# A two-layer hybrid decoder trunk: rotary halves on VectorE, reloads issued by ScalarE, staged compressed probabilities, an early split of w_out's operands

## The chip, the core and the metric

The kernel runs on one core of one Trainium2 chip. What is measured is the device time of one execution in microseconds (us). The core has TensorE (PE, the matmuls; PEld is its weight load), VectorE (DVE), ScalarE (ACT), GpSimd (POOL) and SyncE (SP, which here only issues DMAs). Every engine works through its own queue in order and waits on semaphores for the others.

## What is computed

A trunk of two layers over 512 tokens of width 1024, all in float32. Each layer is a feed-forward half step, a mixing step of three attentions, and another feed-forward half step. Cut to what matters here:

```
h = x + 0.5 * swiglu(rms_norm(x, g1), w1, w3, w2)
u = rms_norm(h, g_mix);  proj = u @ w_in      # columns for A, B and C
A: dilated windows, 3 groups (window, dilation) = (128,1), (512,4), (2048,16); q and k rotated by rope
   o = sum over groups of softmax(lse)[g] * out[g]
B: p_cmp = masked_softmax(q @ kc^T); compressed, selected and window branches;
   q and k rotated by rope; sigmoid gates per branch
C: stick-breaking attention, strictly causal
y = gate0 * (o_a @ w_up_a) + gate1 * (o_b @ w_up_b) + gate2 * (o_c @ w_up_c)
h = h + y @ w_out
h = h + 0.5 * swiglu(rms_norm(h, g2), v1, v3, v2)
```

`apply_rope` turns the first 16 of 64 columns of each head: two products with cos and sin, one difference, one sum.

## The kernel before

All large products run on TensorE in fp32r with split operands: an operand is taken apart into a rounded part (hi) and the rest (lo), and one product is three matmuls, as `acc<-gh,whi`, `acc<-gl,whi`, `acc<-gh,wlo`. Weights are streamed: SP issues the load of a tile `raw` (L352), ScalarE copies it to `whi` (L358), VectorE subtracts to `wlo` (L359), and some tiles later TensorE uses both. A matmul with 512 columns is the usual one; the projection `w_in` runs some with 384.

In mixing, TensorE has two kinds of work. One is that weight stream: `w_in`, the sigmoid gates `w_gate`, then `w_up` and `w_out` (`acc` is their PSUM bank). The other are the small matmuls and transposes of the attentions (`sps` scores, `tps` transposes, `ops` outputs), cut into *units*: generators that `yield` a number of nanoseconds where their next step depends on other engines. `weave` (L426) writes TensorE's order out when the program is built: it keeps a clock of its own estimates, resumes a unit when its due time has come, and otherwise puts the next step of the weight stream (`self.step()`) there as fill. So a `yield` of 3200 means "put about 3200 ns of the weight stream here". TensorE's order is fixed that way; a scheduler then orders VectorE, ScalarE, GpSimd and SP's instructions around it. A unit that is not yet ready (`need`) holds all units behind it in the pending list.

Names that the following needs:

- `rope` (L667 to L681): `ra`, `rb` products with cos and sin, then difference and sum into the first 16 columns. Called on `nata` (A's q and k, 128 partitions), `natk` and `natq` (B's).
- `c_unit` (L843): stick breaking; GpSimd masks `e` and `f` (L851), VectorE scans `f` (L853), GpSimd multiplies `e<-e,f` (L854), TensorE transposes `e`.
- `b_cmp_probs` (L1186 to L1203): the compressed probabilities `ec` of head group g (0 or 1): add the mask, max, subtract, exp, mask again on GpSimd (L1191), sum (L1192), reciprocal, scale on GpSimd (L1196), then transposes.
- The scores of B's other branches are evacuated by VectorE at L1219 (`e,sm<-sps`), normalised by GpSimd at L1223 and transposed.
- `a_unit`: A's attention of one group; softmax sums are put through the small matmuls `tps<-asm,selT` and `tps<-ay,sel`, the group weights `ad`, `ay` (L1438) and `aw` (L1459) come from VectorE, `ea` is scaled (L1443) and transposed, `pa` is its evacuated transpose (L1492).
- The dilated groups store `nata` and `va` to HBM (`ag`) and load them in another layout: `nata<-ag` (L1335) and `va<-ag` (L1336), three reloads in each layer; tile `nat` has two buffers.
- `merge` (L953): `gt` is the stored gate, loaded back by SP (L964), then `gt<-gt,acc` (L969) and `y<-y,gt` (L970). `project_out` splits `y` into `yh` (ScalarE, L988) and `yl` (VectorE, L989) as the operands of `w_out`.

Of the kernel before, what the change touches and what calls it, by code (L numbers as in the profile page):

```python
# [8 lines left out]
F32 = mybir.dt.float32  # L9
F32R = mybir.dt.float32r  # L10
I32 = mybir.dt.int32
AF = mybir.ActivationFunctionType
ALU = mybir.AluOpType
# [42 lines left out]
class Trunk:  # L56
# [610 lines left out]
    def rope(self, x, dil, H):  # L667

        nc = self.nc
        c0 = 4 if dil else 0  # L670
        shp = [128, 4, H, 16]
        cos = self.cos[:, c0:c0 + 4, None, :].to_broadcast(shp)
        sin = self.sin[:, c0:c0 + 4, None, :].to_broadcast(shp)
        ta, tb = self.et("ra"), self.et("rb")
        a = ta[:, :64 * H].rearrange("p (t h d) -> p t h d", t=4, h=H)
        b = tb[:, :64 * H].rearrange("p (t h d) -> p t h d", t=4, h=H)
        xr = x[:, :, :, 0:16]
        nc.gpsimd.tensor_tensor(a, xr, cos, op=ALU.mult)
        nc.gpsimd.tensor_tensor(b, xr, sin, op=ALU.mult)  # L679
        nc.gpsimd.tensor_tensor(x[:, :, :, 0:8], a[:, :, :, 0:8], b[:, :, :, 8:16], op=ALU.subtract)  # L680
        nc.gpsimd.tensor_tensor(x[:, :, :, 8:16], a[:, :, :, 8:16], b[:, :, :, 0:8], op=ALU.add)  # L681

    def st(self, dt, name):
        return self.mp.tile([128, 512], dt, tag="st", name=name, bufs=12)
# [268 lines left out]
    def merge(self, l, mx, r0, o, ready):  # L953
        nc = self.nc
        for mq in range(4):
            ts = []

            def out(j, ts=ts):
                ts.append(self.gt())
                return ts[-1]  # L960

            def load(mq=mq, ts=ts):
                for j in range(2):
                    nc.sync.dma_start(out(j, ts), self.gates[mx, mq][:, j, :])  # L964

            def post(ps, mq=mq, ts=ts):
                for j in range(2):
                    y = self.y[2 * mq + j]
                    nc.vector.scalar_tensor_tensor(ts[j], ts[j], 1.0, ps[j], op0=ALU.add, op1=ALU.mult)  # L969
                    (nc.gpsimd if mx else nc.vector).tensor_tensor(y, y, ts[j], op=ALU.add)  # L970
                if mq == 3:
                    self.done.add(("merge", l, mx))

            if (mx, mq) in self.gates:
                yield self.up(l, r0, mq, o, post, lambda mq=mq: ready(mq), load)
            else:
                yield self.gate(l, mx, mq, out, lambda mq=mq: ready(mq))
                yield self.up(l, r0, mq, o, post)

    def project_out(self, l):  # L980
        nc = self.nc
        yh, yl, h = [], [], []

        def pre():
            for k in range(KD):
                hi = self.gp.tile([128, 512], F32R, tag="gh", name="yh")
                lo = self.gp.tile([128, 512], F32R, tag="gl", name="yl")
                nc.scalar.activation(hi, self.y[k], AF.Copy)  # L988
                nc.vector.tensor_tensor(lo, self.y[k], hi.bitcast(F32), op=ALU.subtract)  # L989
                yh.append(hi)  # L990
                yl.append(lo)

        for mq in range(4):
            def post(ps, mq=mq):
                for j in range(2):
                    m = 2 * mq + j
                    t = self.rp.tile([128, 512], F32, tag="hr", name="hr", bufs=2)
                    nc.sync.dma_start(t, self.spill[:, m, :])
                    hn = self.hp.tile([128, 512], F32, tag="h", name="h")
                    nc.vector.scalar_tensor_tensor(hn, ps[j], 0.5, t, op0=ALU.mult, op1=ALU.add)  # L1000
                    h.append(hn)
                    self.stat_add(m, hn)
                if mq == 3:
                    self.h = h
                    self.done.add(("out", l))

            yield self.proj(self.ins["w_out"][l], 0, (4, 4), mq * 256, lambda: (yh, yl), post,
                            pre=pre if mq == 0 else None,
                            ready=lambda: ("merge", l, 0) in self.done and ("merge", l, 1) in self.done)


# [150 lines left out]
    def b_cmp_probs(self, l, g):  # L1162
        nc = self.nc

        def make(U):
            b, mp = self.b, self.mp
            qt = []
            for p in (2 * g, 2 * g + 1):
                ps = self.trans4(lambda j: b["q"][p][:, j, :])
                t = self.st(F32, "qt")  # L1170
                nc.scalar.activation(t, ps, AF.Copy)
                qt.append(t)
                yield "", 2000 * 0.5
                self.rope(b["q"][p].rearrange("p t (h d) -> p t h d", d=64), False, 2)
            yield "", 2000
            ps = self.sps()
            for i in range(4):
                for p in range(2):
                    self.mm(ps[:, i * 128 + p * 64:i * 128 + (p + 1) * 64], qt[p][:, i * 128:(i + 1) * 128],
                            b["kc"][:, g].rearrange("p a c -> p (a c)"), start=True, stop=True)  # L1180
            e = self.et("ec")
            ev = e.rearrange("p (i r c) -> p i r c", i=4, r=4)
            shp = [128, 4, 4, 32]
            small = lambda n: mp.tile([128, 4, 4], F32, tag=n, name=n, bufs=1)
            mx, ls = small("cmx"), small("cls")
            nc.vector.tensor_tensor(ev, ps.rearrange("p (i r c) -> p i r c", i=4, r=4),  # L1186
                                    self.MC[:, :, None, :].to_broadcast(shp), op=ALU.add)
            nc.vector.tensor_reduce(mx, ev, axis=AX.X, op=ALU.max)
            nc.vector.tensor_tensor(ev, ev, mx[:, :, :, None].to_broadcast(shp), op=ALU.subtract)
            nc.scalar.activation(e, e, AF.Exp)  # L1190
            nc.gpsimd.tensor_tensor(ev, ev, self.MC1[:, :, None, :].to_broadcast(shp), op=ALU.mult)  # L1191
            nc.vector.tensor_reduce(ls, ev, axis=AX.X, op=ALU.add)  # L1192
            nc.vector.tensor_scalar(ls, ls, 1e-30, None, op0=ALU.max)
            nc.vector.reciprocal(ls, ls)
            nc.vector.tensor_tensor(ls, ls, b["g"][:, :, 4 * g:4 * g + 4, 0], op=ALU.mult)
            nc.gpsimd.tensor_tensor(ev, ev, ls[:, :, :, None].to_broadcast(shp), op=ALU.mult)  # L1196
            self.done.add(("cq", l, g))
            yield "", 9200
            ps = self.trans4(lambda i: e[:, i * 128:(i + 1) * 128])
            ph = mp.tile([128, 512], F32R, tag="pch", name="pch", bufs=1)  # L1200
            pl = mp.tile([128, 512], F32R, tag="pcl", name="pcl", bufs=1)
            nc.scalar.activation(ph, ps, AF.Copy)
            nc.vector.tensor_tensor(pl, ps, ph.bitcast(F32), op=ALU.subtract)  # L1203
            b["pc"][g] = ph, pl

        def need():
            d = self.done
            return ("cmp", l) in d and ("bk", l, 1) in d and (g == 0 or ("cqfree", l) in d)

        return Unit(make, need=need, tiles=3)  # L1210
# [119 lines left out]
    def a_reload(self, l, p):  # L1330
        nc = self.nc
        a = self.ain[p]
        a["nat"][0] = self.mp.tile([128, 4, 256], F32, tag="nat", name="nata", bufs=2)
        a["v"][0] = self.mp.tile([128, 2, 4, 128], F32, tag="v2", name="va", bufs=3)[:, 0]
        nc.sync.dma_start(a["nat"][0], self.ag0[p][0])  # L1335
        nc.sync.dma_start(a["v"][0], self.ag0[p][1])  # L1336
        self.done.add(("ag0", l, p))

# [33 lines left out]
    def a_unit(self, l, p):  # L1372
        nc = self.nc

        def make(U):
# [75 lines left out]
            for ip in range(2):  # L1451
                for h in range(2):
                    weigh(0, h, ip)
            yield "", 3200
            ps = self.tps()
            for i in range(4):
                self.mm(ps[:, 0:8], self.sel[:, i, :], y[:, i].rearrange("p c h -> p (c h)"), start=(i == 0),
# [96 lines left out]
    def mix_jobs(self, l):  # L1554
        self.y, self.oc, self.ob, self.oa = [], self.obs.setdefault((l, "c"), []), self.obs.setdefault(l, []), []
        self.gates = {}
        self.gd, self.gld = [], []
        self.cin, self.ain, self.O, self.b, self.ag0 = {}, {}, {}, {"qs": {}, "pc": {}}, {}
        has = lambda *f: (lambda: f in self.done)
        for p in range(3):  # L1560
            yield self.c_inputs(l, p)
        yield from self.b_inputs(l)
        yield from self.a_natural(l)
        for p in range(3):
            yield from self.a_inputs(l, p)
        yield from self.merge(l, 0, 0, {"n": 3, "t": self.oa}, lambda mq: ("adone", l) in self.done)
        yield from self.project_out(l)
# [149 lines left out]
```

## Time and profile before

| | us |
|---|---|
| median of 3 runs | 2831.61 (2830.56 to 2831.69) |
| the profiled execution, its own time | 2828.33 |
| its span in the trace | 2826.6 |
| PE busy | 2777.8 (98%) |
| DVE busy | 1485.0 (53%) |
| ACT busy | 1174.5 (42%) |
| POOL busy | 514.8 (18%) |
| mean granted TensorE clock | 0.996 |

The profiled execution has 1.7 us outside its span, and is 3.3 us below the median. Layer 0's mixing lies between about 450 and 1030 us, layer 1's between 1850 and 2426 us; the rest is feed-forward.

### The profile page before, as it was taken

How to read it: one execution, taken by the hardware profiler on the slowest of the kernel's cores; microseconds unless marked ns; L12 is line 12 of the kernel's file. 1: busy time of each engine (PE TensorE's matmuls, PEld its weight loads, DVE VectorE, ACT ScalarE, POOL GpSimd, SP SyncE). 2: the span in 40 equal slices, each digit the busy share in tenths (PEclk: the TensorE clock that was granted, in tenths of full speed). 3: DMA queues.
4: the chain of work that ended last, by engine and by line, in shares of the span. 5: the costliest groups of instructions: out<-in, count | busy, mean ns of one | idle time of the engine just before them, and what ended most of it. 6: DMA issues, size and time to landing. Idle time of an engine off the chain costs nothing.

```text
span 2826.6 us, 39056 instructions
## 1 busy us (share of the span) xinstructions
PE 2777.8 (98%) x14281; PEld 2387.1 (84%) x14281; DVE 1485.0 (53%) x2923; ACT 1174.5 (42%) x2427; POOL 514.8 (18%) x637
## 2 busy tenths in 40 slices
PE   8999999999999999999999999999999999999998
PEld 7888898888988888888888888988889887888886
DVE  5464346566754565443354543565666446654433
ACT  4333345455644333333233332554556444433332
POOL 2120022133311231110011100231333112311100
PEclk9999999999999999999999999999999999999999
DMA  4333332322233243332333333323222333433332
GB/s 128 97 98 99 117 88 86 95 88 77 69 108 101 86 149 97 97 97 90 104 90 97 97 104 109 88 90 106 77 72 81 97 108 105 128 97 97 97 96 76
DMA packets 298576, 274.58 MB, mean 97 GB/s; under 512 B 14616, under 2 KB 278928, under 8 KB 298384
## 3 DMA queue, kind: packets, MB, share of 16 engines
q1 hardware_dynamic: 292608, 264.49, 31.7%
q10 hardware_dynamic: 5776, 7.60, 0.8%
q8 instruction: 112, 1.84, 0.3%
q14 instruction: 80, 0.66, 0.1%
HBM read 253.69 MB, written 18.35 MB: 96 GB/s over the span
## 4 chain that ended last, share of the span: by engine, by line
PE 92%; DVE 2%; ACT 1%; POOL 1%; issue 1%; DMA 1%; SPq 0%; DVEq 0%; ACTq 0%; POOLq 0%
PE acc L82 64%; PE tps L82 9%; PE sps L82 8%; PE ops L82 8%; PE tps L102 4%; DVE wlo L359 1%; ACT whi L358 0%; DMA gt<-gate 0%; DMA nata<-ag 0%; DMA raw<-in_w_in_dram 0%; POOL ec L1191 0%; POOL e L854 0%; POOL ss L292 0%; DVE ea L1443 0%; POOL rb L679 0%
## 5 line engine op out<-in xcount | busy, mean ns | idle before, releaser
L359 DVE TENSOR_TENSOR wlo<-raw,whi 128x512 fp32r<-128x512 f32 (+3 forms) x944 | 654.1, 700 | 885.2 <-ACT whi L358 835.7
L358 ACT ACTIVATE whi<-raw 128x512 fp32r<-128x512 f32 (+3 forms) x944 | 560.8, 601 | 1031.4 <-PE acc L82 768.8
L82 PE MATMUL acc<-gh,whi 128*128 128x512 f32 x928 | 364.4, 393 | 0.0
L82 PE MATMUL acc<-gh,wlo 128*128 128x512 f32 x928 | 361.6, 390 | 0.0
L82 PE MATMUL acc<-gl,whi 128*128 128x512 f32 x928 | 361.4, 389 | 0.0
L530 POOL TENSOR_TENSOR a<-a,Rb 128x512 f32<-128x512 f32 x88 | 129.6, 1498 | 906.4 <-DVE a L529 877.0
L82 PE MATMUL acc<-hh,whi 128*128 128x512 f32 x704 | 274.2, 390 | 0.0
L82 PE MATMUL acc<-hh,wlo 128*128 128x512 f32 x704 | 273.9, 389 | 0.0
L82 PE MATMUL acc<-hl,whi 128*128 128x512 f32 x704 | 273.9, 389 | 0.0
L82 PEld LDWEIGHTS acc<-gh,wlo 128*128 128x128 f32 x928 | 174.2, 188 | 36.7
L82 PE MATMUL acc<-whi,gh 128*128 128x384 f32 (+2 forms) x576 | 204.4, 355 | 0.0
L82 PEld LDWEIGHTS acc<-gh,whi 128*128 128x128 f32 x928 | 174.4, 188 | 34.9
L82 PEld LDWEIGHTS acc<-gl,whi 128*128 128x128 f32 x928 | 174.4, 188 | 34.7
L82 PE MATMUL acc<-wlo,gh 128*128 128x384 f32 (+2 forms) x576 | 198.3, 344 | 0.5 <-DVE wlo L359 0.5
L82 PE MATMUL acc<-whi,gl 128*128 128x384 f32 (+2 forms) x576 | 197.9, 344 | 0.0
L82 PEld LDWEIGHTS acc<-hh,wlo 128*128 128x128 f32 x704 | 132.1, 188 | 27.5
L82 PEld LDWEIGHTS acc<-hl,whi 128*128 128x128 f32 x704 | 132.2, 188 | 27.3
L82 PEld LDWEIGHTS acc<-hh,whi 128*128 128x128 f32 x704 | 132.1, 188 | 27.3
L82 PE MATMUL acc<-whi,gd 128*128 128x384 f32 x384 | 135.1, 352 | 0.0
L82 PE MATMUL acc<-wlo,gd 128*128 128x384 f32 x384 | 129.5, 337 | 0.0
L82 PE MATMUL acc<-whi,gld 128*128 128x384 f32 x384 | 129.2, 337 | 0.0
L82 PE MATMUL tps<-gh,whi 128*128 128x512 f32 x320 | 124.5, 389 | 0.0
(377 smaller groups left out, 5427.7 us busy)
## 6 DMA issues: line engine op xcount, KB each, us to landing
raw<-in_ffn_w_dram SPq DMA_DIRECT2D x256, 512.0 KB, 3.7
raw<-in_w_in_dram SPq DMA_DIRECT2D x288, 128.0 KB, 2.4
raw<-in_w_gate_dram SPq DMA_DIRECT2D x48, 512.0 KB, 3.5
raw<-in_w_in_dram SPq DMA_DIRECT2D x16, 512.0 KB, 3.6
raw<-in_w_out_dram SPq DMA_DIRECT2D x16, 512.0 KB, 3.6
gate<-gt ACTq DMA_DIRECT2D x28, 256.0 KB, 2.0
gt<-gate SPq DMA_DIRECT2D x28, 256.0 KB, 3.1
raw<-in_w_up_dram SPq DMA_DIRECT2D x16, 384.0 KB, 3.2
```

The costliest lines, as they stand in the source:

```text
L82: self.nc.tensor.matmul(out, lhsT, rhs, start=start, stop=stop, **kw)
L102: self.nc.tensor.transpose(out, in_, self.ident[:n, :n])
L358: nc.scalar.activation(hi, x, AF.Copy)
L359: nc.vector.tensor_tensor(lo, x, hi.bitcast(F32), op=ALU.subtract)
L530: nc.gpsimd.tensor_tensor(v[j], v[j], self.Rb, op=ALU.mult)
```

## The change

Five edits, all in mixing:

1. `rope`: of four GpSimd instructions, the product with sin (L679) and the sum (L681) go to VectorE.
2. `merge` counts its merges per pair of y tiles; after the second one it calls the new `y_split` for that pair. Before, `project_out` made all eight splits as it began.
3. `b_cmp_probs`, for head group 1 only: three new yields (2000, 2500, 2500) between its steps, and the last becomes 4000; group 0 keeps 9200.
4. the reload of `nata` is issued by ScalarE's queue rather than SP's.
5. `a_unit`: a yield of 4200 where 3200 stood, before `tps<-ay,sel`.

```
-        nc.gpsimd.tensor_tensor(b, xr, sin, op=ALU.mult)
+        nc.vector.tensor_tensor(b, xr, sin, op=ALU.mult)
         nc.gpsimd.tensor_tensor(x[:, :, :, 0:8], a[:, :, :, 0:8], b[:, :, :, 8:16], op=ALU.subtract)
-        nc.gpsimd.tensor_tensor(x[:, :, :, 8:16], a[:, :, :, 8:16], b[:, :, :, 0:8], op=ALU.add)
+        nc.vector.tensor_tensor(x[:, :, :, 8:16], a[:, :, :, 8:16], b[:, :, :, 0:8], op=ALU.add)
...
+                self.merged[mq] += 1
+                if self.merged[mq] == 2:
+                    for j in range(2):
+                        self.y_split(2 * mq + j)
...
+    def y_split(self, k):
+        nc = self.nc
+        hi = self.gp.tile([128, 512], F32R, tag="gh", name="yh")
+        lo = self.gp.tile([128, 512], F32R, tag="gl", name="yl")
+        nc.scalar.activation(hi, self.y[k], AF.Copy)
+        nc.vector.tensor_tensor(lo, self.y[k], hi.bitcast(F32), op=ALU.subtract)
+        self.yh[k], self.yl[k] = hi, lo
...
             nc.vector.tensor_reduce(mx, ev, axis=AX.X, op=ALU.max)
+            if g:
+                yield "", 2000
             nc.vector.tensor_tensor(ev, ev, mx[:, :, :, None].to_broadcast(shp), op=ALU.subtract)
             nc.scalar.activation(e, e, AF.Exp)
+            if g:
+                yield "", 2500
             nc.gpsimd.tensor_tensor(ev, ev, self.MC1[:, :, None, :].to_broadcast(shp), op=ALU.mult)
+            if g:
+                yield "", 2500
             nc.vector.tensor_reduce(ls, ev, axis=AX.X, op=ALU.add)
...
-            yield "", 9200
+            yield "", 4000 if g else 9200
...
-        nc.sync.dma_start(a["nat"][0], self.ag0[p][0])
+        nc.scalar.dma_start(a["nat"][0], self.ag0[p][0])
...
-            yield "", 3200
+            yield "", 4200
```

What the order of the instructions becomes is shown at three places.

GpSimd's queue, layer 0, the last unit of stick breaking (`e`, `f`) beside the second rotation of `natk`; before:

```order
L854 TENSOR_TENSOR e<-e,f 128x383
L678 TENSOR_TENSOR ra<-natk,cos 128x256
L851 AFFINE_SELECT f<-f 128x128
L679 TENSOR_TENSOR rb<-natk,sin 128x256
L851 AFFINE_SELECT e<-e 128x128
L680 TENSOR_TENSOR natk<-ra,rb 128x16x8
L681 TENSOR_TENSOR natk<-ra,rb 128x16x8
L854 TENSOR_TENSOR e<-e,f 128x511
```

The same place after:

```order
L854 TENSOR_TENSOR e<-e,f 128x383
L678 TENSOR_TENSOR ra<-natk,cos 128x256
L851 AFFINE_SELECT f<-f 128x128
L851 AFFINE_SELECT e<-e 128x128
L680 TENSOR_TENSOR natk<-ra,rb 128x16x8
L854 TENSOR_TENSOR e<-e,f 128x511
```

Two instructions have left GpSimd's queue ahead of the last `e<-e,f`. VectorE's queue at that place after:

```order
L359 TENSOR_TENSOR wlo<-raw,whi 128x512
L679 TENSOR_TENSOR rb<-natk,sin 128x256
L853 SCALAR_TENSOR_TENSOR f<-f 128x512
L681 TENSOR_TENSOR natk<-ra,rb 128x16x8
L359 TENSOR_TENSOR wlo<-raw,whi 128x512 x2
L766 TENSOR_TENSOR pzl<-tps,pzh 128x384
```

They stand there around the scan of `f` on which that `e<-e,f` waits.

VectorE's queue, layer 0, the compressed probabilities `ec` of head group 1; before:

```order
L1186 TENSOR_TENSOR ec<-sps,MC 128x512
L1188 TENSOR_REDUCE cmx<-ec 128x16
L703 TENSOR_TENSOR qs<-tps,qs 64x512
L1189 TENSOR_TENSOR ec<-ec,cmx 128x512
L1219 ISA e,sm<-sps,Mbig 128x128
L1219 ISA sm 128x1
L703 TENSOR_TENSOR qs<-tps,qs 64x512
L1219 ISA e,sm<-sps,Mbig 128x256
L1219 ISA sm 128x1
L359 TENSOR_TENSOR wlo<-raw,whi 128x384
L1192 TENSOR_REDUCE cls<-ec 128x16
```

After (L1186 has become L1188, L1192 L1200, L1219 L1227):

```order
L1188 TENSOR_TENSOR ec<-sps,MC 128x512
L1190 TENSOR_REDUCE cmx<-ec 128x16
L359 TENSOR_TENSOR wlo<-raw,whi 128x384 x2
L1193 TENSOR_TENSOR ec<-ec,cmx 128x512
L1274 TENSOR_SCALAR gt<-acc,r 128x128 x2
L1200 TENSOR_REDUCE cls<-ec 128x16
L1274 TENSOR_SCALAR gt<-acc,r 128x128
L359 TENSOR_TENSOR wlo<-raw,whi 128x384 x2
```

The score evacuations no longer stand between the steps of `ec`; the first one, L1227, comes ten rows behind L1200. On TensorE, 51 matmuls of 384 columns now stand between `sps<-kc,qt` (which makes `ec`) and the next attention unit, where none stood before.

TensorE's queue, layer 0, the third reload of `nata`; before (SP issues the reload behind the first row's four transposes, and its tile is read by the last eight of the sixteen):

```order
L102 MATMUL tps<-ident,nata 128x128 x4
L82 MATMUL acc<-oh,whi 128x512
L82 MATMUL acc<-ol,whi 128x512
L82 MATMUL acc<-oh,wlo 128x512
L102 MATMUL tps<-ident,nata 128x128 x16
```

After, the four transposes that free the buffer are followed by twelve matmuls `acc<-oh` and `acc<-ol`, and then by:

```order
L102 MATMUL tps<-ident,ea 128x128 x8
L82 MATMUL ops<-pa,va 64x128 x8
L102 MATMUL tps<-ident,nata 128x128 x4
L82 MATMUL ops<-pa,va 64x128 x8
L102 MATMUL tps<-ident,nata 128x128 x12
```

The last eight of the twelve read the reload. ScalarE's queue around its issue, after:

```order
L1368 ACTIVATE qa<-tps 128x512
L358 ACTIVATE whi<-raw 128x512
L1500 ACTIVATE pa<-tps 128x512
L1343 DMA nata<-ag_6374 128x1024
L358 ACTIVATE whi<-raw 128x512
L1500 ACTIVATE pa<-tps 128x512
```

The `pa` ahead of the issue comes from transposes that stand ahead of the freeing four. In a_unit, the matmuls of the weight stream between `tps<-asm,selT` and `tps<-ay,sel` become 27 where 21 stood in the first group, and 21 where 15 stood in the third. The splits `yh`, `yl` (L988, L989) keep their places between the merges on ScalarE and VectorE, but for the last pair.

## Rows read from the trace of the kernel before

**Rows 1.** The page: busy time of each engine (share of the span, instructions).

```profile
PE 2777.8 (98%) x14281; PEld 2387.1 (84%) x14281; DVE 1485.0 (53%) x2923; ACT 1174.5 (42%) x2427; POOL 514.8 (18%) x637
```

**Rows 2.** PE's waits: waiter, whom for, us in total, times, longest.

```profile
PE sps L82 <- DVE sm L1219: 5.8, 8, 1.7
PE tps L102 <- POOL e L854: 4.8, 2, 2.4
PE tps L102 <- DMA nata<-ag: 4.0, 2, 2.2
...
PE tps L102 <- POOL e L1223: 2.7, 2, 1.4
PE tps L82 <- DVE ay L1438: 1.8, 3, 0.8
PE tps L102 <- DVE aw L1459: 1.5, 3, 1.0
PE acc L82 <- DVE gt L969: 1.3, 1, 1.3
```

**Rows 3.** By stretch: length, busy PE, PEld, DVE, ACT, POOL, clock, DMA share, GB/s.

```profile
450.00:1030.00 580.00, 566.42 (x3386) 501.35 (x3385) 344.95 (x828) 287.13 (x686) 141.70 (x216) 1.00 0.32 94
1030.00:1440.00 410.00, 410.00 (x1826) 339.97 (x1825) 193.59 (x293) 141.66 (x229) 52.08 (x36) 1.00 0.33 99
```

**Rows 4.** Timeline of POOL, layer 0, last unit of stick breaking: start, duration.

```profile
584.11 1.18 POOL L679 TENSOR_TENSOR rb<-natk,sin 128x256 f32<-128x256 f32 x1
...
588.13 1.08 POOL L854 TENSOR_TENSOR e<-e,f 128x511 f32<-128x511 f32 x1
```

**Rows 5.** The same stretch, DVE.

```profile
582.00 1.27 DVE L359 TENSOR_TENSOR wlo<-raw,whi 128x512 fp32r<-128x512 f32 x1
...
584.61 1.76 DVE L853 TENSOR_TENSOR_SCAN f<-f 128x512 f32<-128x512 f32 x1
```

**Rows 6.** The same stretch, PE; brackets: idle before it and its releaser.

```profile
589.27 0.55 PE L102 MATMUL tps<-ident,e 128*128 128x128 f32 x3 [2.31 <-POOL e L854]
```

**Rows 7.** Groups by form: count, busy us, mean ns, idle before.

```profile
L679 POOL TENSOR_TENSOR rb<-nata,sin 128x256 f32<-128x256 f32 x18 | 15.8, 878 | 0.0
```

**Rows 8.** The same view, DVE's nearest form of two inputs.

```profile
L359 DVE TENSOR_TENSOR wlo<-raw,whi 128x256 fp32r<-128x256 f32 x16 | 6.7, 418 | 0.1
```

**Rows 9.** Timeline, layer 0, compressed probabilities of group 1, DVE.

```profile
695.65 0.69 DVE L1192 TENSOR_REDUCE cls<-ec 128x16 f32<-128x512 f32 x1 [1.18 <-POOL ec L1191]
```

**Rows 10.** The same stretch, PE.

```profile
697.96 0.50 PE L82 MATMUL sps<-kh,qs 128*128 128x512 f32 x1 [1.64 <-DVE sm L1219]
```

**Rows 11.** Timeline, layer 0, rotation of nata ahead of L1223, POOL.

```profile
735.02 0.77 POOL L681 TENSOR_TENSOR nata<-ra,rb 128x128 f32<-128x128 f32 x1
735.78 1.19 POOL L1223 TENSOR_SCALAR e<-e,sm,glog 128x256 f32<-128x256 f32 x2
```

**Rows 12.** Timeline, layer 1, a_unit of the first group, PE.

```profile
2240.64 0.71 PE L102 MATMUL tps<-ident,ea 128*128 128x128 f32 x3 [1.03 <-DVE aw L1459]
...
2245.73 1.04 PE L102 MATMUL tps<-ident,ea 128*128 128x128 f32 x8
2246.70 0.88 PE L82 MATMUL ops<-pa,va 128*64 128x128 f32 x12
```

**Rows 13.** By stretch, as rows 3: two stretches at half the clock.

```profile
947.20:950.70 3.50, 3.50 (x23) 2.85 (x22) 1.24 (x4) 0.68 (x2) 0.00 (x0) 0.51 0.68 220
...
2240.90:2244.30 3.40, 3.40 (x13) 3.40 (x12) 2.00 (x5) 0.00 (x0) 1.88 (x4) 0.50 0.49 154
```

**Rows 14.** Timeline, layer 0, third reload of nata, PE.

```profile
942.27 0.60 PE L102 MATMUL tps<-ident,nata 128*128 128x128 f32 x4
...
946.62 1.38 PE L102 MATMUL tps<-ident,nata 128*128 128x128 f32 x8 [2.19 <-DMA nata<-ag]
```

**Rows 15.** The same stretch, SP's queue.

```profile
942.95 0.34 SPq L1335 DMA_DIRECT2D nata<-ag  x1
```

**Rows 16.** Timeline, layer 0, the last merges, DVE.

```profile
1008.58 1.38 DVE L969 SCALAR_TENSOR_TENSOR gt<-gt,acc 128x512 f32<-128x512 f32 x2 [1.36 <-DMA gt<-gate]
```

More of the change, by code (lines that the diff above doesn't have):

```diff
@@ L978, in merge @@
                 yield self.up(l, r0, mq, o, post)
+    def y_split(self, k):
[5 more added lines that the diff above has]
+        self.yh[k], self.yl[k] = hi, lo
     def project_out(self, l):
         nc = self.nc
[L982 to L991, printed above, removed]
+        h = []
         for mq in range(4):
@@ L1005, in post @@
                     self.done.add(("out", l))
-            yield self.proj(self.ins["w_out"][l], 0, (4, 4), mq * 256, lambda: (yh, yl), post,
-                            pre=pre if mq == 0 else None,
+            yield self.proj(self.ins["w_out"][l], 0, (4, 4), mq * 256, lambda: (self.yh, self.yl), post,
                             ready=lambda: ("merge", l, 0) in self.done and ("merge", l, 1) in self.done)
@@ L1557, in mix_jobs @@
         self.gd, self.gld = [], []
+        self.merged, self.yh, self.yl = [0] * 4, {}, {}
         self.cin, self.ain, self.O, self.b, self.ag0 = {}, {}, {}, {"qs": {}, "pc": {}}, {}
```

## The prediction

> **What bounds the kernel now.** I read the page first, then PE's waits, then the stretches, then the timelines of single waits. TensorE is busy for 2777.8 of 2826.6 us [rows 1]. Both kernels give it the same matmuls, so an edit can only gain what TensorE idles, or what it runs at half its clock. The feed-forward stretch shows 410.00 busy of 410.00; a mixing stretch shows 566.42 of 580.00 with VectorE at 344.95 and GpSimd at 141.70 [rows 3]. So all that can be had is some 13.6 us in each of two mixing steps, less what no edit touches. The list of PE's waits [rows 2] says what ends it: score banks that VectorE frees late (5.8 us), `e` of stick breaking (4.8), the reload (4.0), `e` of the window branch (2.7), `ay` and `aw` of a_unit (1.8 and 1.5), a gate load (1.3). These seven rows make 21.9 us, and each edit is aimed near one of them. One matmul of 512 columns takes 410.00/1826 = 0.2245 us there [rows 3]; one of 384 columns is put at three quarters of that, 0.168.
>
> **Rotations on two engines.** There are 30 ropes (18 of `nata`, 8 of `natq`, 4 of `natk`), so 60 instructions leave GpSimd for VectorE. The widest group was 18 of 878 ns on GpSimd [rows 7]; for VectorE I take the nearest two-input row of that width, 418 ns [rows 8], and less for the narrow sum. That is some 20 us more for an engine that is 53% busy [rows 1].
>
> *Stick breaking (4.8 us).* GpSimd's multiply began at 588.13 and TensorE had its result at 589.27, 1.14 later [rows 4, 6]. The scan it also needs ended at 584.61 + 1.76 = 586.37 [rows 5]; in between GpSimd was rotating `natk`. With the queue clear the result could come at 586.37 + 1.14 = 587.51, a gain of 1.76. But the order puts `rb` in VectorE's queue ahead of that scan, for 0.42. I take 1.76 - 0.42 = 1.3 a layer, 2.6 in both; ends are 0 (the scan is held as long as GpSimd is relieved) and 3.5. What stays, some 1.0 a layer, is the scan.
>
> *Window branch (2.7 us).* The `e` that TensorE waited for began right behind a rope's sum of 0.77 [rows 11]; that and the `rb` before it, 0.88 by its mean [rows 7], are more than the 1.4 of one wait. They leave, but the units around it shift too, so another rope or cast may stand there. I take two thirds, 1.8; ends 0 and 2.7.
>
> *The price.* VectorE's two new instructions per rope can each wait for GpSimd's half, and behind them stand `wlo`, `pl`, `pzl` and the score evacuations that TensorE waits for. No row shows this wait. Below it is bounded by 0, above by one more wait of the 1.18 that a GpSimd half lasted beside VectorE's work [rows 4], were it to reach TensorE in four or five of the 30 ropes, 5 us. Matmuls have weight tiles in store and VectorE is idle for two fifths of mixing, so I take 1.0.
>
> The rows show the engines holding each other up: `rb` took 1.18 us against a mean of 0.88, while VectorE's `wlo` of 512 columns took 1.27, against 0.84 for twice the one of 256 columns [rows 4, 5, 7, 8]. By the Trainium skill, "SBUF — State Buffer", section "SBUF: two separate sides", a VectorE instruction with two SBUF inputs and a GpSimd instruction that reads SBUF take one shared port pair in turn, the later one waiting whole. That speaks against this edit, since the halves would run one after the other: these stretched rows agree, and by it the two gains above would be near their lower ends and the sum some 4 us smaller (an estimate). I keep the larger values, because even in turn VectorE's half is the shorter one.
>
> **Compressed probabilities in stages (5.8 us).** The cause is one queue. VectorE stood 1.18 us before the sum L1192, because GpSimd's second mask was not done [rows 9]; the score evacuation L1219 stood behind it, and TensorE waited 1.64 for the bank [rows 10]. The order now puts 51 matmuls, 51 x 0.168 = 8.6 us, between the matmuls that make `ec` and the next attention unit, with no evacuation among the `ec` steps. Eight waits make the row, the longest 1.7 [rows 2]; I take 5.0, ends 2.9 (a wait comes back elsewhere in each layer) and 5.8. The cost is fill used earlier: 11000 ns of yields where 9200 stood. I cost it at nothing, since weight matmuls remain behind it up to the last merge, and the later dry place is counted with the reload.
>
> **The yield of 4200 (3.3 us).** It adds 6 matmuls ahead of `tps<-ay,sel`: 6 x 0.168 = 1.0 in the first group and 6 x 0.2245 = 1.35 in the third. The longest wait for `ay` is 0.8 [rows 2], so I take 1.7 of 1.8. `aw` comes after that place; it is helped only because VectorE's scalings of `ea` are done earlier. Its longest wait is 1.03 [rows 12]; I take 1.0 of 1.5, ends 0 and 1.5. Together 2.7.
>
> **The reload (4.0 us).** In before the freeing transposes began at 942.27, SP issued at 942.95, TensorE had the tile at 946.62, having stood 2.19 [rows 14, 15]: 4.35 us from the first of the four to the use. After, the order has between the two, beside the four, 12 matmuls (2.7), 16 other transposes at 0.97/8 = 0.12 (1.9) and 16 `pa` matmuls at 0.88/12 = 0.07 (1.1) [rows 12]: 5.7 us and the four. That is over 1 us more than 4.35, so the stall of both layers goes: 4.0. This row of transposes without weight matmuls needs its banks evacuated one after the other, which I put at 0.3 a layer, ends 0 and 1.0. So 3.4. ScalarE pays for six issues; SP's took 0.34 each [rows 15], so 2.0 us on an engine with far more idle, with a few `whi` behind each, of which some are in store. Zero for TensorE.
>
> It is the position that pays, not the issuing engine: SP's queue held the reload back for TensorE's transposes, not for other issues. By the Trainium skill, "Trainium Kernel Development and Optimization", section "Key Constraints", transfers issued from SP and ScalarE share the same 16 DMA engines, and issuing from several engines saves issue time only. On that rule alone edit 4 is worth nothing and the stall would stay; it is a rival below.
>
> **Splitting y.** The scheduler had the splits between the merges already; ScalarE's and VectorE's rows barely move. Worth 0. The one wait there, 1.3 us in layer 0 alone, is VectorE's for the load of a gate [rows 2, 16]; the change moves other transfers around it, so I count it neither gone nor doubled: plus or minus 1.3.
>
> **The clock.** Two stretches of mixing ran at a granted clock of 0.50 and 0.51, that is 1.2 of 2.4 GHz [rows 13]: one began 0.6 us after the reload's wait of 2.19, the other 0.3 us after the wait for `aw` of 1.03. The second held 13 matmuls in 3.40 us, where 13 x 0.168 = 2.2, so 1.2 lost; the first held small ones, and loses at most half of 3.5; I take 0.8. Without the waits ahead I expect both gone: 2.0, ends 2.0 and -2.0 (two others appear).
>
> **Sum.** 2.6 + 1.8 + 5.0 + 2.7 + 3.4 + 2.0 - 1.0 = 16.5. The profiled execution took 2828.33 itself, so 2811.8 for one like it; the median of the runs stands 3.3 above that execution, so 2815.1, forecast 2815. Upper ends of all terms make 22 to 25 us (2807); lower ends all at once make no gain.
>
> **Rivals.** (a) *The ropes take turns.* VectorE holds its queue for GpSimd's halves; the gains in stick breaking and window branch go (4.4) and the price is 5 rather than 1. Gain 16.5 - 8.4 = 8.1, 2823.5. For it: the stretched rows. Against: GpSimd loses 15.8 us in one form and about as much again in the other forms, and is only 18% busy [rows 1, 7].
> (b) *The reload doesn't profit* (it does not do what it says): the transfer lands later behind `w_up` and gate loads now issued beside it, or ScalarE reaches its issue late. Then 3.4 and 0.8 go: 12.3, 2819.3. Against: over 1 us of spare by the order.
> (c) *Slower.* Each of the 60 moved instructions holds VectorE as the `wlo` was held, 1.27 - 0.84 = 0.43 us, and all of it reaches TensorE through late `wlo` and score banks: 60 x 0.43 = 26 in place of 1.0, so 26 - 17.5 = 8.5 lost, 2840. It decides from 17.5/60 = 0.29 us each reaching TensorE. Against: VectorE idles 235 of 580 us in mixing [rows 3].
> (d) *The waits only move*: every staged piece finds another late bank; within 0.2% of before, 2828.
>
> **How the numbers follow.** Forecast 0.67, (a) 0.14, (b) 0.10, (d) 0.05, (c) 0.04. About 0.2%, 5.7 us, is what a measurement of this kernel tells from no change: faster means below 2826. That holds for the forecast, for (b) and for most of (a), 0.86, and I take off 0.02 for what the listing of waits doesn't show: faster 0.84, same 0.11, slower 0.05. The range goes from 2804, a little below all upper ends, to 2828, which leaves out (c) and half of (d).
>
> **What would show it.** In the profile after: PE's waits for the score bank near 697 us and for `nata<-ag` are gone; `e` of stick breaking stays with about 1.0 us a layer; `ay` and `aw` under 1 us in all; no stretch at half clock near 947 or 2241; ropes' `rb` on VectorE near 0.4 us. I am wrong if VectorE's new instructions show long waits for GpSimd with `wlo` or L1227 behind them, if TensorE waits in the dry row of transposes before the third group, or if new waits stand where the 51 matmuls were taken from.

## The result: 22 us faster, with the score wait as long as before

| | before | changed |
|---|---|---|
| median, us | 2831.09 (2827.19 to 2834.06, 6 runs) | 2808.82 (2806.47 to 2809.73, 6 runs) |
| the profiled execution, its own time | 2828.33 | 2808.57 |
| span | 2826.6 | 2806.9 |

The ratio is 0.9923, with a 95% interval of 0.9912 to 0.9933: 0.8% faster, 22.3 us by the medians. Forecast were 16.5 us less than before, 2815, in a range of 2804 to 2828; the time lies in the range and the direction was right.

The page of the changed kernel answers to [rows 1]; columns are busy us, share and instructions.

```profile
PE 2772.0 (99%) x14281; PEld 2385.3 (85%) x14281; DVE 1498.6 (53%) x2983; ACT 1176.3 (42%) x2427; POOL 486.2 (17%) x577
```

TensorE has the same 14281 instructions; 60 have gone from POOL to DVE, and cost 13.6 us more there and 28.6 less on POOL (the prediction had put some 20 more on DVE). PE's waits in the changed kernel answer to [rows 2]; columns are us in total, times, longest; the first row of the list, a load at the start of the kernel (6.9), is left out:

```profile
PE sps L82 <- DVE sm L1227: 5.8, 8, 1.8
PE tps L82 <- POOL ss L292: 4.2, 1, 4.2
PE acc L82 <- DVE gt L969: 1.4, 1, 1.4
PE tps L102 <- POOL e L854: 1.3, 2, 0.7
PE ops L82 <- DVE pcl L1211: 0.9, 2, 0.4
PE tps L102 <- ACT natc L1039: 0.8, 2, 0.4
PE tps L102 <- DVE qa L1366: 0.7, 2, 0.3
```

Gone from the list are `nata<-ag` (4.0), `e` of the window branch (2.7), `ay` (1.8) and `aw` (1.5); `e` of stick breaking fell from 4.8 to 1.3. In their place stands `qa` with 0.7. (`qa` are the evacuated transposes of `nata`; `ss` are the sums of squares of a norm at the start, outside mixing, 3.6 us before; `pcl` and `pch` are the low and high part of the transposed `ec`, `pl`, `ph`, `pzl` and `pzh` those of the transposed `e`; `natc` belongs to the stick-breaking branch.) The score banks, which the largest term of the forecast meant, wait 5.8 us as before. They do it elsewhere, though. The stretches of the two mixing steps, to set beside [rows 3] (length, busy PE, PEld, DVE, ACT, POOL, clock, DMA share, GB/s), changed:

```profile
450.00:1030.00 580.00, 573.53 (x3425) 509.37 (x3424) 356.96 (x865) 290.20 (x690) 134.10 (x191) 1.00 0.32 96
...
1850.00:2426.00 576.00, 571.19 (x3415) 507.36 (x3414) 357.35 (x864) 290.72 (x687) 135.41 (x188) 1.00 0.33 97
```

Layer 1 before:

```profile
1850.00:2426.00 576.00, 563.68 (x3375) 499.90 (x3374) 344.41 (x828) 286.45 (x685) 141.27 (x215) 1.00 0.32 94
```

TensorE's idle in these stretches of time went from 13.6 to 6.5 us in layer 0 and from 12.3 to 4.8 in layer 1. Now the place of the longest score wait, layer 0, timelines of PE, DVE and POOL (start, duration, then in brackets the idle before and its releaser):

```profile
722.35 0.50 PE L82 MATMUL sps<-kh,qs 128*128 128x512 f32 x1 [1.83 <-DVE sm L1227]
...
724.85 0.67 PE L82 MATMUL acc<-whi,gd 128*128 128x384 f32 x1
725.32 0.52 PE L82 MATMUL acc<-whi,gld 128*128 128x384 f32 x1
```

```profile
719.74 0.60 DVE L359 TENSOR_TENSOR wlo<-raw,whi 128x384 fp32r<-128x384 f32 x1
720.26 0.69 DVE L798 TENSOR_TENSOR ol<-of,oh 128x512 fp32r<-128x512 f32 x1
720.87 0.35 DVE L1274 TENSOR_SCALAR gt<-acc,r 128x128 f32<-128x128 f32 x1
721.13 0.69 DVE L679 TENSOR_TENSOR rb<-nata,sin 128x256 f32<-128x256 f32 x1
721.74 0.55 DVE L1227 CUSTOM_DVE_ANT_0 e<-sps,Mbig 128x384 f32<-128x384 f32 x1
```

```profile
720.74 0.80 POOL L678 TENSOR_TENSOR ra<-nata,cos 128x256 f32<-128x256 f32 x1 [0.81 <-ACT nata L1273]
```

The evacuation L1227 that would free the bank stands in DVE's queue behind a head output's `ol`, a scaling of A's `v` (which the program names `gt` there), and `rb`, the half of the rotation that the change put on DVE. `rb` lasted 0.69 us; it began while POOL's `ra` ran (720.74 to 721.54), and the last section shows what that does. TensorE stands 1.8 us here, and up to 726.6 us its matmuls of 384 columns then begin 0.32 us apart or more, where 0.17 is usual: half the clock for a while.

The stretches of [rows 13] at half the clock are gone. The first two rows here are the start of the kernel and the piece around the end of the half clock behind that wait, the third is what now follows layer 0's last reload (columns as before):

```profile
29.00:33.80 4.80, 4.80 (x13) 3.83 (x14) 1.52 (x7) 0.21 (x1) 0.00 (x0) 0.50 0.35 109
724.80:727.20 2.40, 2.40 (x10) 2.40 (x10) 1.41 (x3) 1.54 (x4) 0.77 (x1) 0.59 0.71 186
941.60:945.10 3.50, 3.50 (x28) 2.96 (x28) 2.16 (x9) 1.90 (x8) 0.00 (x0) 1.00 0.13 45
```

### The profile page after: what moved, and what is told of

Its sections match the earlier page's. It is cut to its first block, busy times and chain, and to the rows that moved or that the text cites. A ratio compares the mean times of both kernels' runs of the same rounds, so it can differ in the third digit from the quotient of the medians.

```text
span 2806.9 us, 39062 instructions
## 1 busy us (share of the span) xinstructions
PE 2772.0 (99%) x14281; PEld 2385.3 (85%) x14281; DVE 1498.6 (53%) x2983; ACT 1176.3 (42%) x2427; POOL 486.2 (17%) x577
## 4 chain that ended last, share of the span: by engine, by line
PE 95%; DVE 2%; issue 1%; POOL 1%; ACT 1%; DMA 0%; ACTq 0%; DVEq 0%; POOLq 0%
PE acc L82 66%; PE tps L82 9%; PE sps L82 8%; PE ops L82 8%; PE tps L102 4%; DVE wlo L359 0%; DMA gt<-gate 0%; POOL e L854 0%; POOL ss L292 0%; POOL ra L678 0%; DVE e L1227 0%; DMA gr<-in_cmp_pe_v_dram 0%; ACT e L1229 0%; PE acc L102 0%; DVE rb L679 0%
```

## The experiments

Theory: TensorE's order, as the yields lay it out, decides when each wait can be covered; the engine that issues a transfer or does half a rotation matters little ("position"). Rivals: the issuing engine ends the reload's wait ("engine"); the rotation halves give with one hand and take with the other ("taking turns"). Edits 1, 3, 4 and 5 were each put alone on the kernel before; edits 1, 2, 4 and 5 were each taken alone out of the changed kernel. The changed kernel without edit 3 was not run. All ratios are to the kernel before, run on the same chip. On the chips of the three groups of runs that kernel took 2831.56, 2828.61 and 2829.56 us, so kernels of different groups are compared by their ratios, whose intervals reach 3.5 to 4 us to either side where a kernel ran four or five times. The short diffs give the whole edit.

### Edit 3 alone on the kernel before

```
+            if g:
+                yield "", 2000
...
+            if g:
+                yield "", 2500
...
+            if g:
+                yield "", 2500
...
-            yield "", 9200
+            yield "", 4000 if g else 9200
```

> The kernel before with the staged yields alone (edit 3). Theory 'position': the wait for the third reload ends because these yields move TensorE's order, whoever issues the reload. Then `nata<-ag`, 4.0 us in before, is under 0.5 here though SP still issues it, the score waits near 690 to 698 us (2.8 in each layer) are gone, `e` of the window branch (2.7) mostly too, and the kernel is 8 to 13 us faster than before, 2818 to 2823. Theory 'engine': the reload's wait ends because ScalarE issues it; then 4.0 us of it stay here and the gain is 3 to 7 us, 2824 to 2828. On the new score wait of 1.8 us near 720 us in the changed kernel: if VectorE's halves of the rotation make it, it is under 0.5 here, since all of rope is on GpSimd; if the shift of units makes it, it is 1.2 or more here too.

Measured: 2812.90 us (2809.43 to 2814.24) against 2831.56; ratio 0.9931 (0.9918 to 0.9943). PE's waits of this kernel:

```profile
PE tps L102 <- POOL e L854: 4.6, 2, 2.3
PE tps L82 <- POOL ss L292: 3.6, 1, 3.6
PE sps L82 <- DVE sm L1225: 3.5, 6, 1.0
PE tps L102 <- ACT pa L1498: 1.2, 2, 0.6
...
PE tps L102 <- DVE aw L1465: 0.4, 2, 0.2
```

No row for `nata<-ag` is left, although SP issues the reload; `ay` is gone, although the yield is 3200; `e` of the window branch is gone, although GpSimd does all rotations. The gain, 18.7 us (19.5 by the ratio), is more than either theory allowed, and the ratio's interval overlaps that of the whole change (0.9912 to 0.9933). "Position" holds and was too modest. The score waits fell from 5.8 to 3.5. The new wait near 722 us is there, with GpSimd's rotation:

```profile
723.63 0.50 PE L82 MATMUL sps<-kh,qs 128*128 128x512 f32 x1 [0.99 <-DVE sm L1225]
```

That is between the two readings of the expectation: 0.99 of the 1.83 us comes from the shift of the units, and some 0.8 from something else in the changed kernel; the run without the split rotation, below, says what.

### Edit 4 alone on the kernel before

```
-        nc.sync.dma_start(a["nat"][0], self.ag0[p][0])
+        nc.scalar.dma_start(a["nat"][0], self.ag0[p][0])
```

> The kernel before with the reload issued by ScalarE alone (edit 4); TensorE's order is that of before, word for word. Theory 'position': the wait of 4.0 us for `nata<-ag` stays between 3.5 and 5, and the time is that of before within 2 us, 2829 to 2833. Theory 'engine': it falls under 1, and the time by 4 to 6 us, 2825 to 2827.

Measured: 2833.14 us (2829.34 to 2834.80) against 2831.56; ratio 1.0004 (0.9995 to 1.0013). The waits for the reload:

```profile
PE tps L102 <- DMA nata<-ag: 4.2, 2, 2.3
```

and the view of the issuing line: the six issues, and from issue to landing.

```profile
L1335 ACTq DMA_DIRECT2D nata<-ag x6: 326/326/326, 797.9 to 2346.6; - x6
...
DMA to landing us min/median/max: 3.2/3.3/3.6
```

Nothing was gained: the transfer landed as late as by SP (3.2, 3.3 and 3.5 us in before), and TensorE waited as long. "Engine" has fallen.

### Edit 5 alone on the kernel before

```
-            yield "", 3200
+            yield "", 4200
```

> The kernel before with the yield of 4200 alone (edit 5). The waits for `ay` (1.8) go under 0.3. If the longer yield also lets VectorE reach `aw` early, the wait for `aw` (1.5) and the half clock near 2241 us go too: 4 to 5 us faster, 2826 to 2827. If `aw` was not helped by it but by the other edits, 1.5 to 2 us faster, 2829, with half a clock still granted near 2241. `nata<-ag` stays near 4.0 in both.

Measured: 2826.87 us (2823.83 to 2829.66) against 2831.56; ratio 0.9985 (0.9976 to 0.9994), 4.2 us by the ratio. `ay` is no longer in the list; `aw` stays but is spread:

```profile
PE tps L102 <- DVE aw L1459: 1.5, 4, 0.6
```

The gain is that of the first case, the mechanism is not: `aw` did not get shorter in sum, its longest wait fell from 1.0 to 0.6, and layer 1's clock from 2238 to 2245 us was granted in full (1.00). What was gained in waits are 1.8 us of `ay` and 0.6 of `pa`. Whether the stretch at half clock was gained by the edit stays open: the same trace has two that the trace before lacks, at 1982 us behind a wait of 2.29 for `e` (0.54) and at 2340 behind one of 1.76 for the reload (0.52).

### Edit 1 alone on the kernel before

```
-        nc.gpsimd.tensor_tensor(b, xr, sin, op=ALU.mult)
+        nc.vector.tensor_tensor(b, xr, sin, op=ALU.mult)
...
-        nc.gpsimd.tensor_tensor(x[:, :, :, 8:16], a[:, :, :, 8:16], b[:, :, :, 0:8], op=ALU.add)
+        nc.vector.tensor_tensor(x[:, :, :, 8:16], a[:, :, :, 8:16], b[:, :, :, 0:8], op=ALU.add)
```

> The kernel before with the rotation's halves on VectorE alone (edit 1); TensorE's order is that of before. Theory 'less queue': `e` of stick breaking falls from 4.8 to 1.3 us and `e` of the window branch from 2.7 to under 1, the score waits stay near 5.8: 4 to 6 us faster, 2825 to 2827. Theory 'taking turns eats it': the score waits grow by 3 us or more as VectorE's queue is held by the halves, and the time stays within 2 us of before, 2829 to 2833. In either, VectorE's `rb` of 128x256 begun beside GpSimd's `ra` lasts until after that `ra` ends, 0.7 to 1.0 us, against 0.4 where GpSimd is idle.

Measured: 2826.61 us (2824.93 to 2828.47) against 2831.56; ratio 0.9984 (0.9975 to 0.9992), 4.5 us by the ratio. Its waits:

```profile
PE sps L82 <- DVE sm L1219: 6.7, 10, 1.7
...
PE tps L82 <- DVE ay L1438: 2.9, 4, 1.0
PE tps L102 <- DVE pzl L766: 1.5, 2, 0.8
PE tps L102 <- POOL e L854: 1.4, 2, 0.7
```

"Less queue" gave 3.4 at stick breaking and 2.7 at the window branch, and `aw` fell by 1.1; 0.9 was taken back at the score banks, 1.1 at `ay`, 1.5 at `pzl` and 0.6 at `pa`, which fits VectorE's fuller queue. Both theories are at work and the first was the larger in this order of TensorE. VectorE's `rb` of `nata` took 0.41 to 0.91 us, 0.71 in the median; 0.7 to 1.0 had been expected beside `ra`.

### The changed kernel with the reload issued by SP

The edit is that of edit 4, reversed.

> The changed kernel with the reload issued by SP again (edit 4 undone); TensorE's order is that of the changed kernel. Theory 'position': TensorE still has no wait for `nata<-ag` and the time is that of the changed kernel within 2 us, 2807 to 2811. Theory 'engine' in a weaker form (in the new order SP's queue would hold `raw` and gate loads behind the reload): 3 to 6 us slower, 2812 to 2815, with waits for `raw`, `whi` or `gt`.

Measured: 2809.99 us (2808.19 to 2810.53), ratio 0.9927 (0.9914 to 0.9941). No wait for `nata<-ag`. The landing times, of this kernel:

```profile
DMA to landing us min/median/max: 3.3/4.3/4.4
```

and of the changed one, by ScalarE:

```profile
DMA to landing us min/median/max: 3.2/4.0/4.4
```

By the ratios edit 4 is worth about 1 us, which this measurement can't tell from nothing. The transfers land later in the new order, whoever issues them, and TensorE does not wait for them.

### The changed kernel with the yield of 3200

The edit is that of edit 5, reversed.

> The changed kernel with the yield of 3200 (edit 5 undone). The staged yields alone already ended the wait for `ay`. If the edits overlap there, this is slower than the changed kernel by 0 to 2 us, 2808 to 2811, with waits for `aw` and `pa` of under 2 us; if they add up as they do on the kernel before (4.2 us there), 2812 to 2814.

Measured: 2809.83 us (2808.41 to 2810.67), ratio 0.9929 (0.9916 to 0.9941): 1.7 us by the ratios, within their intervals. `pa` (1.2) and `aw` (0.4) wait, `ay` doesn't: what edit 5 ends, edit 3 had mostly ended.

### The changed kernel with all of rope on GpSimd

The edit is that of edit 1, reversed.

> The changed kernel with all of rope on GpSimd (edit 1 undone). `e` of stick breaking goes back from 1.3 to 4.6 us; the score wait near 720 us falls from 1.8 to about 1.0 and the one near 757 from 0.7 to about 0.5, in each layer, if VectorE's halves make up that difference. Net: the rotation on two engines is worth 0.5 to 3 us here against 4 us on the kernel before, 2809 to 2812. If the score wait does not fall, the halves are not its cause and the net is 3 to 5 us, 2812 to 2814.

Measured: 2809.33 us (2807.30 to 2809.48), ratio 0.9925 (0.9913 to 0.9938), some 0.6 us off the changed kernel by the ratios. Its waits:

```profile
PE tps L102 <- POOL e L854: 4.7, 2, 2.4
...
PE sps L82 <- DVE sm L1227: 3.5, 6, 1.0
```

The score waits fall to 3.5: VectorE's halves make 2.3 of their 5.8 us. They pay 3.4 at stick breaking, so 1.1 us of waits is left to edit 1: in the new order, it is as a whole worth nothing that could be measured. The half clock does not decide it: this trace has two such stretches, at 589 and 1975 us behind the waits for `e`, the changed kernel's has one, at 724. No row for `e` of the window branch is left here, so with edit 3 in, edit 1 is not needed for it.

### The changed kernel with all splits of y at the start of w_out

```
-                self.merged[mq] += 1
-                if self.merged[mq] == 2:
-                    for j in range(2):
-                        self.y_split(2 * mq + j)
...
+        def pre():
+            for k in range(KD):
+                self.y_split(k)
...
+                            pre=pre if mq == 0 else None,
```

> The changed kernel with all eight splits of y made as `project_out` begins (edit 2 undone). By the prediction's working it is worth nothing: 2807 to 2811, the one wait at the first matmul of w_out staying that of VectorE for a gate load, between 0 and 2.7 us in one of the layers. If the early split matters, TensorE waits for `yh` or `yl` there in both layers and the kernel is 2 to 4 us slower.

Measured: 2809.27 us (2807.18 to 2810.19), ratio 0.9926 (0.9914 to 0.9939). Edit 2 is worth nothing that could be measured, and no wait for `yh` or `yl` is in the list.

### The longer sum without the stages, on the kernel before

```
-            yield "", 9200
+            yield "", 11000 if g else 9200
```

> The kernel before with one yield of 11000 for head group 1 where 9200 stood: the same sum as edit 3, without its stages. TensorE's order at the third reload stays that of before. If the gain of the staged yields comes from the stages, which hold the next units back and so move TensorE's order, this is worth under 2 us, 2829 to 2832, with `nata<-ag` near 4.0 and the score waits near 690 to 698 us as before. If it comes from the 1800 ns more, 8 us or more faster, under 2824.

Measured: 2829.89 us (2826.65 to 2831.60) against 2829.56, ratio 0.9998 (0.9989 to 1.0007). `nata<-ag` waits 4.3 us, the score banks 8.0. So it is the stages and not the 1800 ns more: in `b_cmp_probs` the flag that lets the next unit start is set behind the new yields, so TensorE does its w_in matmuls first, and every later unit meets another piece of the weight stream. That the flag is what matters is read from the program; one long yield ahead of the flag, without stages, was not run.

### The changed kernel with the split rotation for `natk` and `natq` only

```
+    def rope(self, x, dil, H, eng=None):
...
+        eng = eng or nc.gpsimd
...
+        eng.tensor_tensor(b, xr, sin, op=ALU.mult)
...
+        eng.tensor_tensor(x[:, :, :, 8:16], a[:, :, :, 8:16], b[:, :, :, 0:8], op=ALU.add)
```

`natk` and `natq` are called with VectorE, `nata` without.

> The changed kernel with rope on two engines for `natk` and `natq` alone; all four instructions for `nata` are on GpSimd. Theory: VectorE's halves pay at stick breaking (the wait for `e` near 587 us stays at 0.7 in each layer) and cost at the score banks, by those of `nata`. Then the score waits go back to 3.5 us in all (1.0 near 720, 0.5 near 757) and the kernel is 2 to 4 us faster than the changed one, 2805 to 2807. If the score waits stay at 5.8, the halves of `nata` are not their cause and the time stays at 2808 to 2810.

Measured: 2803.86 us (2802.37 to 2807.68, 4 runs), ratio 0.9910 (0.9897 to 0.9924), against 0.9923 (0.9912 to 0.9933) of the changed kernel. By the ratios it is 3.7 us faster than the changed kernel, within the 2 to 4 that were expected, and its median is the lowest of all here; the intervals overlap, so that it beats the changed kernel is likely and not settled. The trace shows the mechanism that was foreseen:

```profile
PE sps L82 <- DVE sm L1228: 3.4, 6, 1.0
PE tps L102 <- POOL e L855: 1.3, 2, 0.7
```

### That kernel, with group 0 staged too

```
-            if g:
-                yield "", 2000
+            yield "", 2000
...
-            yield "", 4000 if g else 9200
+            yield "", 4000
```

The two yields of 2500 lose their `if g` as well.

> The kernel rope_split_for_b_only with the staged yields for head group 0 too. If staging is good in itself, the waits near 614 to 619 us (score bank 0.3, `pch` 0.2, `pcl` 0.4 in each layer) go, and it is 1 to 2 us faster than rope_split_for_b_only. If it is good only by where it happens to put the later units, these go but others come: within 1 us or slower.

Measured: 2804.58 us (2803.09 to 2808.32, 4 runs), ratio 0.9913 (0.9899 to 0.9926). The waits for `pch` and `pcl` are gone, and `e` of the window branch is back, so the second reading of the expectation holds:

```profile
PE tps L102 <- POOL e L1229: 2.9, 2, 1.5
PE sps L82 <- DVE sm L1225: 2.3, 4, 0.6
```

### That kernel, with 10800 for group 0, which is not staged

```
-            yield "", 4000 if g else 9200
+            yield "", 4000 if g else 10800
```

> The kernel rope_split_for_b_only with 10800 where 9200 stood for head group 0, not staged. The transposes of `ec` of group 0 come 1.6 us later; the waits for `pch` and `pcl` (0.6 us a layer) stay or move. Within 1.5 us of rope_split_for_b_only.

Measured: 2806.77 us (2803.72 to 2807.72), ratio 0.9915 (0.9902 to 0.9929). `pch` waits more (1.4), `pcl` and the score banks less (0.7 and 2.4), and `aw` waits again (0.9). By the ratios it is 1.4 us slower than the kernel without this edit, by the medians 2.9, and the intervals overlap: the expectation holds within the spread, and the edit only moves waits about.

## Why the prediction was right, and where its sizes were not

*The bound.* Right: TensorE's work is unchanged, and the gain is TensorE's idle and half clock. Of its waits in mixing, 14.6 us left the list: 3.5 of `e`, 4.0, 2.7, 1.8 and 1.5 of [rows 2], 1.9 of three small ones (0.7 of `ec`, 0.6 each of `pl` and `pa`), less 0.7 of `qa` and 0.1 of `gt`. Without the clock the forecast's terms add up to 14.5. That the two agree so closely is luck: the score waits less the price, taken as 4.0 together, came to nothing, and what made it up was 0.8 more at stick breaking, 0.9 at the window branch, 0.6 at `ay` and `aw`, and the small waits, which no term names. The span fell by 19.7, although the start of the kernel, which no edit touches, was about 1 us longer in this trace (its stretch from 29.00 to 33.80 us ran at 0.50 throughout, before at 0.64 on average). The rest I put down to half clock and to slower first matmuls behind each wait; how it divides was not measured.

*Staged yields: a mis-sized term, and the wrong reason.* The forecast gave them 5.0 us of score waits, with a lower end of 2.9. The waits at 690 to 698 us did go, but others came at 720 and 757 us: with edit 3 alone the sum fell to 3.5, a gain of 2.3, and edit 1's halves brought it back to 5.8. But the same edit moved every unit behind it, and alone it took 18.7 us, beside 22.3 for the whole: the reload's wait, `e` of the window branch, `ay`, most of `aw`, and the two stretches at half clock of [rows 13]. The prediction had all these effects in its sum, and had read from the order that TensorE's place of the reload moved, but it put them down to the edits that are named after them. Its sentence on the reload, "It is the position that pays, not the issuing engine", was right, and both runs on the issue show it; what made the position was edit 3, which it did not see. Why the wait for `ay` went in that run, with the same 21 matmuls ahead of it, stays open.

*Rotations.* At stick breaking 1.7 us a layer were gained against 1.3, the wait left being 0.7 against 1.0; there VectorE's `rb` of `natk` began at 585.29, after its `ra` had ended at 584.71, and took 0.51. The window branch, sized 1.8, gave 2.7, and either edit alone, 1 or 3, ends it. The price, taken as 1.0 with an end of 5, was 2.3 at the score banks, and on the kernel before 4.1 by the list of edit 1 alone (0.9, 1.1, 1.5 and 0.6). So rival (a) was partly right: VectorE's queue was held by its half beside GpSimd's, and in the new order this cost 2.3 of the 3.4 us that the other gave. The time hides it, because edit 3 brought more than its term. The "price" was sized by a guess that weight tiles cover it, where the instruction that waited behind `rb` was a score evacuation that nothing covers. Two of the prediction's own signs speak to this: `rb` on VectorE was not near 0.4 us but 0.70 in the median for `nata`, and L1227 stood behind it, which it had named as a sign of being wrong.

*The yield of 4200.* 2.7 in the sum; 4.2 alone, 1.7 beside edit 3 by ratios that can't tell it from nothing. *The reload* went as worked out: 4.0 gone, and in the row of transposes before the third group, which the prediction had named as dry, 0.7 new at the banks (0.6 was taken). *The split of y* was worth 0, as said. *The gate load* waited 1.4 in one layer, as before.

*The clock.* The two stretches named went, as expected, and a new one came behind the score wait at 722 us, as the lower end of that term allowed. How much of this is the change and how much the execution, single traces don't say. Before had a stretch at 0.50 where no edit reaches, which is gone too (columns as in [rows 3]):

```profile
1790.30:1793.70 3.40, 3.40 (x13) 3.40 (x13) 1.59 (x8) 0.96 (x4) 0.00 (x0) 0.50 0.33 76
```

And the same wait is followed by half clock in one execution and not in another: behind the score wait near 722 us in the changed kernel (1.83), but not with the reload issued by SP (1.80), and not in layer 1 (1.60); behind `e` near 589 us with edit 3 alone (2.32), but not in before (2.31).

The sum of the four single edits on the kernel before is 18.7 + 4.7 + 5.0 - 1.6 = 26.8 us by medians, against 22.3 for the whole. The difference of 4.5 is within what the intervals allow; that the edits overlap is shown by the lists of waits, where edits 1 and 3 each end `e` of the window branch alone, and edits 3 and 5 each end `ay`.

## What to carry to other kernels

Where one engine is the bound and its order is laid out by yields or a planner's clock, an edit to one unit can move all later ones; its worth is read from the whole order, and attributing it needs each edit run alone. Before giving half of a chain to a second engine, look at what stands behind the new instruction in that engine's queue and whether its reader has cover: here the same split paid where a masked product waited and cost where a score bank did. When a wait is said to end, look for the row with the same name elsewhere: the sum of the score waits, not the place, said what was gained, and the lists of the single edits said by which.

## What the runs showed of the hardware

The halves of a rotation on VectorE and GpSimd mostly did not run side by side. In the changed kernel POOL and DVE show, at another rope of layer 0:

```profile
755.47 0.74 POOL L678 TENSOR_TENSOR ra<-nata,cos 128x256 f32<-128x256 f32 x1
```

```profile
755.52 0.98 DVE L679 TENSOR_TENSOR rb<-nata,sin 128x256 f32<-128x256 f32 x1
```

`ra` ends at 756.21 and `rb` at 756.50, 0.29 us behind it, where the fastest `rb` of this size took 0.41 in all. So it is in 14 of the 18 rotations of `nata`: `rb` begins while `ra` runs, lasts 0.68 to 1.00 us and ends 0.28 or 0.29 behind it. In two of the other four `rb` began 0.22 us ahead of `ra` and took 0.52 and 0.53; in two `ra` had ended, and it took 0.41. It looks as if the later one had waited for the earlier. This is what the Trainium skill, "SBUF — State Buffer", section "SBUF: two separate sides", says of two such instructions, and the trace agrees; the prediction had named the rule and kept the larger values all the same.

The issuing engine made no difference that shows to a transfer's landing: 3.3 us by SP's median and by ScalarE's in the old order, 4.3 and 4.0 in the new one. That, too, agrees with the sentence on issuing that the prediction took from the Trainium skill, "Trainium Kernel Development and Optimization", section "Key Constraints".
